# Token loads of the last operands: other tiles, ScalarE's queue, three groups

## The chip, the cores and the metric

One core of a Trainium2 chip runs the kernel. The metric is the device time of one execution in microseconds (us). TensorE (PE) multiplies, VectorE (DVE), ScalarE (ACT) and GpSimd (POOL) work on tiles in on-chip memory, and SyncE (SP) issues transfers (DMAs) between it and HBM. Each engine works through its own queue in order.

## What is computed

A decoder block on x of 2048 tokens by 1024, in fp32: a mixing layer (stick-breaking attention and pooling) and then a gated feed-forward layer. The change lies in the second:

```python
h = rmsnorm(x, g_ffn_pre[l]) * (1.0 + scale_f) + shift_f
f = (jax.nn.silu(h @ w_gate[l]) * (h @ w_up[l])) @ w_down[l]
x = x + gate_f * rmsnorm(f, g_ffn_post[l])
```

w_gate and w_up are 1024 by 2816, w_down is 2816 by 1024.

## The kernel before

Every fp32 product is made of three matmuls on fp32r pairs: a tile is split into a high part (ScalarE's cast) and a low part (VectorE's difference), and the three helper lines L72, L73, L74 multiply high by high, low by high and high by low. In most splits here (`split_by_bank`) ScalarE also copies the rounded value into a PSUM bank (L1176), and VectorE takes the low part from there (L1177).

The products with w_gate and w_up are two-level Strassen-like schemes of seven products each. Four *passes* (`inner`, q = 0 to 3, names p1 to p4) make some products for 11 column chunks j each; a chunk is seven steps of six matmuls, in the banks a, e, f, b, h, i, d. Their results go to HBM (`pd`, L1385). Then 11 *main* chunks (`gate_up`) follow, twelve steps of twelve matmuls each, which fetch the passes' products again (`px`, L1433) and add them. A main step's names: t2, t3 or b22 for the token operand (the trace prints t and b), 0 or 1 for the half of the tokens, g or u for gate or up. The first main chunk takes t2 of both halves (four steps), t3 of half 0, b22 of half 0, t3 of half 1 (`t31_g`, `t31_u`), b22 of half 1.

The main token operands are made beside pass four, in a side generator that gets one turn per step. `main_operands` loads, for each of eight row blocks u, three parts (n = 1, 3, 0) of the stored tokens h2d (`token_part`, L1622, 256 KB), subtracts and adds them on GpSimd (L1692) and splits the results into t2, t3 and b22 of half 0 and t2 of half 1. `rest_operands` loads parts 1 and 3 of the four row blocks of half 1, subtracts on GpSimd (L1726) and splits into t3 and b22 of half 1. Loaded tiles are named hs{block}_{i}_{n}: hs8_3_0 is part 0 of row block 3 of half 1; two tiles of `rest_operands` lie in one wide tile, hs_wide.

Scratch tiles have tags with a fixed number of buffers: "gs" has 3, "cu" 2, "v2", "v3", "u4" and "p1" one each ("u2", "v2", "u3", "v3" hold sums in the main chunks). A new tile of a tag waits until the readers of the one before are done. In pass four each chunk's gate weights come in two row halves, g and g2, that GpSimd adds (L1347).

The order of the compute engines' instructions is the program's own. SyncE's transfers are put in an order by the scheduler, which judges by its own model when a tile is free; the chip then follows that order strictly. Each transfer signals one of eight counters (DMAHW0 to DMAHW7), in turn over both issuing queues, and a transfer is issued only when the one before on its counter has landed.

## Time and profile before

| what | us |
|---|---|
| median of 3 runs (2202.04 to 2202.92) | 2202.14 |
| the profiled execution | 2203.83 |
| its span, first to last instruction | 2202.0 |
| TensorE busy in the span | 2172.7 |
| pass four, first to last step | about 1315 to 1413 |
| main chunks | 1414.6 to about 1765 |

Busy times are sums over instructions of one engine. An engine that is not the bound may be idle at no cost. A wait is put down to the instruction that released it last. In rows of a timeline stand the start, the duration, engine, line, operation, written tile, read tiles and the shape; in brackets the idle time ahead and its releaser. SPq rows are issues of transfers, not the transfers.

### The profile page before, as it was taken

The page shows a single profiled execution, that of the slowest core. Times are in us where ns is not written, and L with a number is a line of the kernel's source. Part 1 is how long each engine was busy: PE and PEld are TensorE (multiplying, and loading weights), DVE is VectorE, ACT ScalarE, POOL GpSimd, SP SyncE. Part 2 cuts the span into 40 slices and gives each one's busy share as a digit, 9 for nine tenths or more (in the row PEclk, how much of TensorE's full clock was granted, in tenths as well). Part 3 has the DMA queues.
Part 4 walks back from the last instruction along what each step waited for, and adds up shares of the span by engine and source line. Part 5 has one row for each costly group of instructions (what it writes and reads, how often), then busy time and mean ns, then how long its engine had stood idle before and what let it go on. Part 6 is the DMA issues. An engine that isn't in the chain of part 4 may idle for free.

```text
span 2202.0 us, 34273 instructions
## 1 busy us (share of the span) xinstructions
PE 2172.7 (99%) x10349; PEld 1796.3 (82%) x10349; DVE 1673.7 (76%) x2552; ACT 1356.3 (62%) x2796; POOL 1215.6 (55%) x1700
## 2 busy tenths in 40 slices
PE   8999999999999999999999999999999999999998
PEld 6888888888888888887878878788888888888887
DVE  7874499999999966547778878788778765577566
ACT  5334589989989854547766657554444444455444
POOL 1352267787879965547788677566666520032003
PEclk9999999999999999999999999999999999999999
DMA  8986886634343445668889889899999897679553
GB/s 315 335 290 208 285 218 176 172 90 119 113 136 97 149 163 193 196 216 286 287 297 334 271 273 285 276 337 327 302 314 297 308 323 259 211 245 327 187 199 118
DMA packets 365573, 524.78 MB, mean 238 GB/s; under 512 B 24198, under 2 KB 203978, under 8 KB 357836
## 3 DMA queue, kind: packets, MB, share of 16 engines
q1 hardware_dynamic: 362828, 521.02, 72.3%
q8 instruction: 82, 1.34, 0.3%
q10 hardware_dynamic: 2560, 1.58, 0.3%
q14 instruction: 103, 0.84, 0.1%
HBM read 350.01 MB, written 172.49 MB: 237 GB/s over the span
## 4 chain that ended last, share of the span: by engine, by line
PE 52%; POOL 2%; DVE 2%; DMA 1%; ACT 1%; issue 1%; SPq 0%; DVEq 0%; POOLq 0%; ACTq 0%
PE dn0p L74 3%; PE dn0p L73 3%; PE dn0p L72 3%; PE dn1p L73 3%; PE dn1p L72 3%; PE dn1p L74 3%; PE t_g L72 2%; PE t_u L72 2%; PE t_g L73 2%; PE t_u L73 2%; PE t_g L74 2%; PE t_u L74 2%; PE mix L72 1%; PE mix L73 1%; PE mix L74 1%
## 5 line engine op out<-in xcount | busy, mean ns | idle before, releaser
L953 POOL TENSOR_TENSOR w<-sg,pr 128x512 f32<-128x512 f32 (+2 forms) x320 | 306.3, 957 | 46.4 <-DVE pr L948 15.4
L948 DVE TENSOR_TENSOR_SCAN pr<-pr,carry,begin 128x512 f32<-128x512 f32 x192 | 244.0, 1271 | 0.0
L932 ACT ACTIVATE sg<-z 128x512 f32<-128x512 f32 (+2 forms) x320 | 183.7, 574 | 51.0 <-PE z L930 41.5
L63 DVE TENSOR_TENSOR wtl<-wt,wth 128x512 fp32r<-128x512 f32 (+1 forms) x320 | 189.6, 592 | 17.9 <-ACT wth L62 15.7
L62 ACT CAST wth<-wt 128x512 fp32r<-128x512 f32 (+1 forms) x320 | 183.0, 572 | 10.4 <-PE wt L964 10.4
L934 ACT ACTIVATE pr<-z 128x512 f32<-128x512 f32 (+2 forms) x320 | 183.2, 572 | 0.0
L964 PE MATMUL wt<-ident,w 128*128 128x128 f32 x1088 | 172.3, 273 | 1.6 <-POOL pr L944 1.1
L964 PEld LDWEIGHTS wt<-ident,w 128*128 128x128 f32 x1088 | 134.1, 140 | 32.8 <-POOL pr L944 1.9
L1486 ACT ACTIVATE sa<-sa 128x512 f32<-128x512 f32 x88 | 54.7, 632 | 160.8 <-DVE sa L1485 158.1
L979 PE MATMUL av<-wth,vt 128*128 128x512 f32 (+1 forms) x320 | 126.1, 394 | 0.9 <-ACT o L984 0.8
L63 DVE TENSOR_TENSOR g0p_l<-g0p,g0p_h 128x512 fp32r<-128x512 f32 x77 | 59.6, 775 | 79.8 <-ACT g0p_h L62 79.8
L73 PE MATMUL dn0p<-w0p_l,g0p_h 128*128 128x512 f32 x308 | 119.8, 389 | 0.0
L74 PE MATMUL dn0p<-w0p_h,g0p_l 128*128 128x512 f32 x308 | 119.8, 389 | 0.0
L72 PE MATMUL dn0p<-w0p_h,g0p_h 128*128 128x512 f32 x308 | 119.8, 389 | 0.0
L929 PE MATMUL z<-kt,qt 128*128 128x512 f32 (+2 forms) x320 | 118.7, 371 | 0.7 <-ACT pr L934 0.6
L980 PE MATMUL av<-wtl,vt 128*128 128x512 f32 (+1 forms) x320 | 117.8, 368 | 1.3 <-DVE wtl L63 1.2
L930 PE MATMUL z<-kt,qt 128*128 128x512 f32 (+2 forms) x320 | 116.9, 365 | 0.0
L73 PE MATMUL dn1p<-w1p_l,g1p_h 128*128 128x512 f32 x292 | 113.6, 389 | 0.0
L74 PE MATMUL dn1p<-w1p_h,g1p_l 128*128 128x512 f32 x292 | 113.6, 389 | 0.0
L72 PE MATMUL dn1p<-w1p_h,g1p_h 128*128 128x512 f32 x292 | 113.6, 389 | 0.0
L62 ACT CAST g0p_h<-g0p 128x512 fp32r<-128x512 f32 x77 | 48.0, 623 | 105.3 <-PE dn0p L73 92.5
L945 DVE TENSOR_TENSOR_SCAN pr<-pr,zero,begin 128x128 f32<-128x128 f32 (+3 forms) x128 | 111.2, 871 | 1.7 <-ACT pr L934 1.7
(852 smaller groups left out, 7151.6 us busy)
## 6 DMA issues: line engine op xcount, KB each, us to landing
pd<-p_c SPq DMA_DIRECT2D x176, 256.0 KB, 4.9
px<-pd SPq DMA_DIRECT2D x42, 1024.0 KB, 7.3
hs<-h2d SPq DMA_DIRECT2D x78, 256.0 KB, 4.7
wc<-in_w_cond_dram SPq DMA_DIRECT2D x32, 512.0 KB, 7.4
qt<-qd SPq DMA_DIRECT2D x64, 256.0 KB, 4.1
kt<-kd SPq DMA_DIRECT2D x96, 128.0 KB, 3.2
vt<-vd SPq DMA_DIRECT2D x48, 256.0 KB, 4.0
wd<-in_w_down_dram SPq DMA_DIRECT2D x44, 256.0 KB, 5.5
```

The source lines that it names most:

```text
L62: nc.scalar.copy(hi, src)
L63: low.tensor_tensor(lo, src, raw(hi), ALU.subtract)
L72: nc.tensor.matmul(ps, lh, rh, start=first and i == 0, stop=False)
L73: nc.tensor.matmul(ps, lh, rl, start=False, stop=False)
L74: nc.tensor.matmul(ps, ll, rh, start=False, stop=last and i == n - 1)
L929: nc.tensor.matmul(z[:, 0:L], qt[:, 0, i * P:(i + 1) * P], keys, start=True, stop=False)
L932: nc.scalar.activation(sg[:, 0:L], z[:, 0:L], AF.Sigmoid, scale=0.125)
L934: nc.scalar.activation(pr[:, 0:L], z[:, 0:L], AF.Sigmoid, scale=-0.125)
L948: nc.vector.tensor_tensor_scan(keys, keys, begin, carry, ALU.mult, ALU.bypass)
L953: nc.gpsimd.tensor_tensor(w[:, 0:L], sg[:, 0:L], pr[:, 1:L + 1], ALU.mult)
L964: nc.tensor.transpose(wt[:, i * P:(i + 1) * P], wss[u][i][:, b * P:(b + 1) * P], ident)
L979: nc.tensor.matmul(av[:, lo0:], vb, wh[:, lo0:], start=first, stop=False)
```

## The change

Three things are edited. The last chunk's gate halves of pass four go to the tiles v3 and v2 instead of the two "cu" tiles. The last row block of `main_operands` (u = 7) takes "cu", "cu" and "gs" instead of three "gs" tiles, and its part 0 is loaded by ScalarE. The eight loads of `rest_operands` are issued by ScalarE instead of SyncE, and in three groups (row blocks 0 and 1; 2; 3) instead of all at the start; one more turn is left free ahead of the last row block's subtraction.

```diff
                 if m == NQ * HF - 1:
-                    st["g"], st["g2"] = (ft("cu", f"{name}_{n}") for n in ("g", "g2"))
+                    st["g"], st["g2"] = (ft(tag, f"{name}_{n}") for n, tag in (("g", "v3"), ("g2", "v2")))
...
-    def token_part(n, T0, tag, i, t=None):
+    def token_part(n, T0, tag, i, t=None, queue=nc.sync):
         t = ft(tag, f"hs{T0}_{i}_{n}", (P, HK, P)) if tag else t
-        nc.sync.dma_start(t, h2d[T0 + n % 2 * HK + i][:, n // 2 * HK:(n // 2 + 1) * HK, :])
+        queue.dma_start(t, h2d[T0 + n % 2 * HK + i][:, n // 2 * HK:(n // 2 + 1) * HK, :])
...
-            raw[u, n] = token_part(n, u // HK * NTS, tag, u % HK)
+            raw[u, n] = token_part(n, u // HK * NTS, tag, u % HK, queue=nc.scalar if u == 7 and not n else nc.sync)
...
-            tags = ("cu", "cu", "v2") if u in (1, 3, 5) else ("gs",) * 3
+            tags = ("cu", "cu", "gs" if u == 7 else "v2") if u % 2 else ("gs",) * 3
...
-        for i, (tag, tag2) in enumerate((("cu", "gs"), (None, "gs"), (None, "gs"), ("u4", "p1"))):
-            b12.append(token_part(1, NTS, tag, i, wide[:, (i - 1) % 2]))
-            b22.append(token_part(3, NTS, tag2, i))
-        yield
-        yield
-        for k in range(HK + 2):
-            if k < HK:
+        tags = (("cu", "gs"), (None, "gs"), (None, "gs"), ("u4", "p1"))
+        for k in range(-2, HK + 2):
+            for i in {-2: (0, 1), -1: (2,), 1: (3,)}.get(k, ()):
+                b12.append(token_part(1, NTS, tags[i][0], i, wide[:, (i - 1) % 2], nc.scalar))
+                b22.append(token_part(3, NTS, tags[i][1], i, queue=nc.scalar))
+            if k == HK - 1:
+                yield
+            if 0 <= k < HK:
                 nc.gpsimd.tensor_tensor(b12[k], b22[k], b12[k], ALU.subtract)
```

SyncE's queue late in pass four, before. The rows are pass-four sums on their way out (pd), weights of pass four (p4_10) and of main chunk 0 (g_0), and token loads:

```order
L1334 DMA p4_10_g2_17960<-in_w_gate_dram 128x4x128
L1385 DMA pd0_158<-p4_6_c00_17853 128x512
L1385 DMA pd1_159<-p4_6_c11_17868 128x512
L1385 DMA pd0_158<-p4_6_c10_17885 128x512
L1622 DMA hs8_3_1_18076<-h2d15_135 128x512
L1622 DMA hs8_3_3_18078<-h2d15_135 128x512
L1445 DMA g_0_320_18010<-in_w_gate_dram 128x8x128
L1385 DMA pd1_159<-p4_6_c01_17923 128x512
L1340 DMA p4_10_32_17958<-in_w_up_dram 128x8x128
L1622 DMA hs8_0_1_18346<-h2d12_132 128x512
L1385 DMA pd0_158<-p4_7_c00_17971 128x512
L1385 DMA pd1_159<-p4_7_c11_17986 128x512
```

The same stretch now:

```order
L1622 DMA hs8_3_3_18078<-h2d15_135 128x512
L1385 DMA pd0_158<-p4_6_c00_17853 128x512
L1385 DMA pd1_159<-p4_6_c11_17868 128x512
L1385 DMA pd0_158<-p4_6_c10_17885 128x512
L1334 DMA p4_10_g2_17960<-in_w_gate_dram 128x4x128
L1445 DMA g_0_320_18010<-in_w_gate_dram 128x8x128
L1385 DMA pd1_159<-p4_6_c01_17923 128x512
L1340 DMA p4_10_32_17958<-in_w_up_dram 128x8x128
L1385 DMA pd0_158<-p4_7_c00_17971 128x512
L1385 DMA pd1_159<-p4_7_c11_17986 128x512
L1385 DMA pd0_158<-p4_7_c10_18002 128x512
```

The pair hs8_3_1, hs8_3_3 has gone ahead of the sums of chunk 6 (its first load stands four rows higher still), g2 has taken its place ahead of g_0, and hs8_0_1 and hs8_3_0 have left SyncE. The first gate half, p4_10_g, now stands some 350 rows higher, in pass one.

ScalarE at the start of main chunk 0, before (b0g0 and b0u0 copy products of px00 into banks; t3_1h is the high part of a row block of t3 of half 1; L1486 is the silu):

```order
L1176 COPY rounded_18338<-g_0_s3_h_18335 128x512
L1480 COPY b0g0_0_18390<-px00_0_18285 128x512
L1169 CAST u_0_s3_h_18398<-u_0_320_18057 128x512
L1176 COPY rounded_18401<-u_0_s3_h_18398 128x512
L1486 ACT_TABLE_LOAD
L1486 ACTIVATE sa110_0_18394<-sa110_0_18394 128x512
L1480 COPY b0u0_0_18419<-px00_0_18285 128x512
L1169 CAST t3_1h_18341<-hs8_0_1_18346 128x4x128
```

And now, with the counters that each row waits for:

```order
L1622 DMA hs8_0_1_18346<-h2d12_132 128x512 [waits DMAHW0_49]
L1622 DMA hs8_0_3_18348<-h2d12_132 128x512 [waits DMAHW4_49]
L1622 DMA hs_wide_18345<-h2d13_133 128x512 [waits DMAHW5_49]
L1622 DMA hs8_1_3_18351<-h2d13_133 128x512 [waits DMAHW7_49]
L1622 DMA hs_wide_18345<-h2d14_134 128x512 [waits DMAHW0_49]
L1622 DMA hs8_2_3_18366<-h2d14_134 128x512 [waits DMAHW2_49]
L1480 COPY b0g0_0_18386<-px00_0_18285 128x512 [waits DVE_49]
...
L1480 COPY b0u0_0_18415<-px00_0_18285 128x512 [waits DMAHW1_49]
L1622 DMA hs8_3_1_18421<-h2d15_135 128x512 [waits DMAHW6_49,DVE_49]
L1622 DMA hs8_3_3_18423<-h2d15_135 128x512 [waits DMAHW0_49]
L1169 CAST t3_1h_18341<-hs8_0_1_18346 128x4x128 [waits PE_49,Pool_49]
```

Six loads stand ahead of b0g0 and two ahead of the first cast of t3_1h. On the counters: hs8_0_1 has DMAHW2 (GpSimd's L1727 waits for it there), the first half of px00 has DMAHW0.

VectorE in chunk 0, before (t30_g and t30_u are the results of t3 of half 0; t3_1l and b22_1l the low parts of t3 and b22 of half 1):

```order
L1177 TENSOR_TENSOR u_0_s4_l_18488<-u_0_s4_18266,rounded_18490 128x512
L1177 TENSOR_TENSOR t3_1l_18342<-hs_wide_18345,rounded_18495 128x4x128
L63 TENSOR_TENSOR b22_1l_18344<-hs8_1_3_18351,b22_1h_18343 128x4x128
L1506 TENSOR_TENSOR t30_g_0_18466<-t30_g_0_18466,u2g0_0_18392 128x512
L1485 TENSOR_TENSOR sa120_0_18519<-t30_g_0_18466,px10_0_18372 128x512
L1485 TENSOR_TENSOR sa220_0_18521<-t30_g_0_18466,px10_0_18372 128x512
L1516 TENSOR_TENSOR u2g0_0_18392<-b1g0_0_18516,u2g0_0_18392 128x512
L1177 TENSOR_TENSOR t3_1l_18342<-hs8_3_1_18356,rounded_18525 128x4x128
```

And now:

```order
L1506 TENSOR_TENSOR t30_g_0_18466<-t30_g_0_18466,u2g0_0_18388 128x512
L1485 TENSOR_TENSOR sa120_0_18512<-t30_g_0_18466,px10_0_18368 128x512
L1485 TENSOR_TENSOR sa220_0_18514<-t30_g_0_18466,px10_0_18368 128x512
L1516 TENSOR_TENSOR u2g0_0_18388<-b1g0_0_18509,u2g0_0_18388 128x512
L1177 TENSOR_TENSOR t3_1l_18342<-hs_wide_18345,rounded_18519 128x4x128
L63 TENSOR_TENSOR b22_1l_18344<-hs8_1_3_18351,b22_1h_18343 128x4x128
L1506 TENSOR_TENSOR t30_u_0_18496<-t30_u_0_18496,u2u0_0_18417 128x512
L1512 TENSOR_TENSOR cu0_0_18544<-t30_u_0_18496,px10_0_18368 128x512
L1489 TENSOR_TENSOR t30_u_0_18496<-t30_u_0_18496,px10_0_18368 128x512
L1490 TENSOR_TENSOR sa220_0_18514<-sa220_0_18514,t30_u_0_18496 128x512
L1516 TENSOR_TENSOR u2u0_0_18417<-b1u0_0_18541,u2u0_0_18417 128x512
L1177 TENSOR_TENSOR t3_1l_18342<-hs8_3_1_18421,rounded_18551 128x4x128
```

The low part of row block 3 stood behind t30_g's sums; now it stands behind t30_u's five rows too.

## The prediction

> **What bounds the kernel now.** First the head of the page: who is busy, and for how long.

> ```profile
> span 2202.0 us, 34273 instructions
> PE 2172.7 (99%) x10349; PEld 1796.3 (82%) x10349; DVE 1673.7 (76%) x2552; ACT 1356.3 (62%) x2796; POOL 1215.6 (55%) x1700
> ```

> TensorE is idle for 2202.0 - 2172.7 = 29.3 us in all, so the change can win only what of this lies at its place. The profiled execution took 2203.83 us, 1.8 outside its span and 1.7 above the median 2202.14; I work with differences and add them to the median. 0.2% of it, 4.4 us, is about what a measurement of this kernel tells from no change.

> Second, TensorE's waits between 1360 and 1460 us (the end of pass four and the first main chunk), and its timeline there (start, duration, in brackets the idle time ahead):

> ```profile
> PE t_g L72 <- DVE p_c L1389: 1.5, 1, 1.5
> PE hp L72 <- DVE p_c L1389: 0.2, 1, 0.2
> ...
> 1409.48 0.39 PE L74 MATMUL bp<-yap4h,p_g_l 128*128 128x512 f32 x1
> 1410.05 0.47 PE L72 MATMUL hp<-v32p4h,p_s_h 128*128 128x512 f32 x1 [0.18 <-DVE p_c L1389]
> 1411.58 0.39 PE L72 MATMUL ip<-v14p4h,p_u_h 128*128 128x512 f32 x1
> 1412.72 0.39 PE L74 MATMUL ip<-v14p4h,p_u_l 128*128 128x512 f32 x1
> 1414.63 0.47 PE L72 MATMUL t_g<-t_0h,g_s_h 128*128 128x512 f32 x1 [1.53 <-DVE p_c L1389]
> 1417.46 0.39 PE L72 MATMUL dp<-y22p,p_s_h 128*128 128x512 f32 x1
> ```

> These two waits are the whole target. Starts without a wait are 0.227 us apart (1411.58 to 1412.72 is 5 of them). From 1409.48 to 1417.46 stand 25 matmuls, 5.68 us without a wait; they took 7.98. The most to be won is **2.30 us**, 0.10%.

> Third, the chain of waits through this place, and SyncE's queue:

> ```profile
> 1387.77 6.61 DMA p<-in_w_up_dram
> 1394.45 7.37 DMA g<-in_w_gate_dram
> 1401.95 1.29 POOL g L1451
> ...
> 1407.27 0.63 ACT t_1h L1169
> ...
> 1408.61 0.70 DVE t_1l L1177
> ...
> 1413.81 0.69 DVE p_c L1389
> ```
> ```profile
> 1373.58 0.65 SPq L1334 DMA_DIRECT2D p_g<-in_w_gate_dram  x1
> ...
> 1383.50 3.08 SPq L1622 DMA_DIRECT2D hs<-h2d  x2
> 1386.67 0.39 SPq L1445 DMA_DIRECT2D g<-in_w_gate_dram  x1
> ...
> 1405.89 1.69 SPq L1622 DMA_DIRECT2D hs<-h2d  x2
> 1407.67 0.39 SPq L1445 DMA_DIRECT2D u<-in_w_up_dram  x1
> ...
> 1413.49 1.30 SPq L1433 DMA_DIRECT2D px<-pd  x2
> ```

> SyncE's in-order queue is the cause: token loads that wait for their tiles (1383.50, 1405.89) hold the weight loads behind them. The gate weights of chunk 0 land at 1401.95, GpSimd's queue is late by that, the fourth row block's cast (L1169) with it, VectorE's low part at 1408.61 (L1177) holds the sums behind it, and the last of these (L1389, 1413.81) frees what t_g waits for.

> **The change, part by part.**

> *Row block 3 into other tiles, last gate weights into v3 and v2.* The pair of token loads now takes the place of the gate halves (1373.58), and the second half waits for v2, free some 3 us later. Nothing behind them waits for a token load any more; each load goes when VectorE has read its own tile, which for g, the one the chain runs through, is this row:

> ```profile
> 1389.21 0.68 DVE L1177 TENSOR_TENSOR p_g_l<-p_g,rounded 128x512 fp32r<-128x512 f32 x1
> ```

> So g goes near 1390 instead of 1394.45 and, with the same 7.4 us, lands at 1397.4; the up weights ahead of it (1387.77) go earlier still. The fourth row block is cast 4 to 5 us earlier, at about 1403, ahead of the sums it held. **-2.30 us**, both waits gone. The first gate half, free of any wait, moves to pass one in SyncE's order: one 0.4 us issue and 256 KB there; I cost it at nothing, and give +-1 us for the shift of the counters of all loads after it.

> *Token loads on ScalarE's queue.* Nine issues. The nearest rows: ScalarE's loads in pass one (issue in ns; then KB and us to landing), the landing of all loads of that line, of all token loads (4.7), of the token loads between 1400 and 1440 us, and of px; then a gap of ScalarE, and where GpSimd's queue stands:

> ```profile
> L1344 ACTq DMA_DIRECT2D p<-in_w_up_dram x2: 375/515/655, 1006.4 to 1017.0; - x2
> ...
> DMA to landing us min/median/max: 3.3/5.2/8.0
> ...
> p<-in_w_up_dram ACTq DMA_DIRECT2D x2, 256.0 KB, 6.0
> ...
> hs<-h2d SPq DMA_DIRECT2D x78, 256.0 KB, 4.7
> ...
> DMA to landing us min/median/max: 5.2/5.5/5.8
> ...
> px<-pd SPq DMA_DIRECT2D x4, 512.0 KB, 7.2
> ...
> 1394.94 0.59 ACT L1394 COPY p1p<-ap 128x512 f32<-128x512 f32 x1 [3.52 <-PE ap L74]
> ...
> 1408.43 1.30 POOL L1459 TENSOR_TENSOR g_s<-g,g 128x512 f32<-128x512 f32 x1 [1.20 <-PE fp L73]
> ```

> At about 0.4 us each: the one for row block 3 goes into the gap of 3.52 us ahead of 1394.94. Six stand ahead of b0g and two ahead of the first t3 cast. None is free there, because the queue behind each waits, and because the sixth, hs8_2_3, uses the counter of the first, hs8_0_1, and so waits until that has landed, with b0g (L1480) behind it. This is the new wait.

> ScalarE gets to the six at about 1414.7: g_s at 1408.43 keeps its wait for TensorE, then three GpSimd operations of 1.3 us (1412.3), then two casts with their copies, 2.4. If the first lands 4.7 us later (1419.4), the sixth issue ends at 1419.8 and VectorE's sa, behind b0g, starts 0.6 after: S = 1420.4. Bounds: the six issues alone, 2.3 us, S = 1417.6; a landing of 8.0, S = 1423.7. I take 4.7, the median of 78 loads of the same form, between ScalarE's 3.3 at best and its 6.0.

> *One step later.* In the new order the low part t3_1l of row block 3, the last that t31_g needs, stands behind five more VectorE rows. The rows of before:

> ```profile
> 1419.59 0.59 ACT L1480 COPY b0g<-px 128x512 f32<-128x512 f32 x1 [1.61 <-DMA px<-pd]
> ...
> 1420.21 0.69 DVE L1485 TENSOR_TENSOR sa<-b0g,px 128x512 f32<-128x512 f32 x1
> ...
> 1436.40 0.69 DVE L1177 TENSOR_TENSOR t_1l<-hs,rounded 128x512 fp32r<-128x512 f32 x1
> ...
> 1437.92 0.69 DVE L1506 TENSOR_TENSOR t_u<-t_u,u2u 128x512 f32<-128x512 f32 x1
> ...
> 1441.25 1.31 DVE L63 TENSOR_TENSOR b_1l<-hs,b_1h 128x512 fp32r<-128x512 f32 x1
> ...
> 1437.86 0.39 PE L72 MATMUL t_g<-t_1h,g_s_h 128*128 128x512 f32 x1
> ...
> 1420.00:1430.00 10.00, 10.00 (x46) 8.29 (x45) 8.54 (x15) 9.81 (x18) 1.67 (x2) 1.00 1.12 351
> ```

> Before, t3_1l ends at 1437.09, 16.88 us after sa's start and 0.77 before TensorE comes: that is all the slack. The five rows are those from 1437.92 to 1441.25, 3.33 us. So it now ends at S + 20.21. VectorE and ScalarE, busy 8.5 and 9.8 of 10 us there, give nothing back. TensorE, 2.30 earlier, wants it at 1437.86 - 2.30 + 0.23 = 1435.79 (the low part is read by the second matmul). The stall is S - 1415.6, the **net S - 1417.9**.

> *Sum.* -2.30 + (1420.4 - 1415.6) = -2.3 + 4.8 = **+2.5 us**: 2202.14 + 2.5 = 2204.6. Bounds: -0.3 (S 1417.6) to +5.8 (S 1423.7); -2.3 if the later place is covered.

> *What moves past what.* SyncE loses the nine issues, so px00 goes as soon as bp has read its tile, near 1409.8 instead of 1413.49; the 6 us it took (1413.49 to 1419.59) lets it land near 1416, ahead of S. px10, which b1g and sa wait for, lands near 1430: about 7.3 MB from 1409.8 at the 374 GB/s of the row below; it is wanted at about S + 12.4 = 1432.8, after the sums ahead of it. gf's load, now earlier in SyncE's order, waits for hs_wide's readers with only chunk-1 loads behind it, wanted 20 us later.

> ```profile
> 1400.00:1410.00 10.00, 9.87 (x44) 7.85 (x42) 4.41 (x8) 2.67 (x5) 6.42 (x5) 1.00 0.45 146
> 1410.00:1420.00 10.00, 8.43 (x36) 6.57 (x37) 7.57 (x13) 4.80 (x10) 6.95 (x6) 1.00 1.01 374
> ```

> These rows (last columns: clock, DMA share, GB/s) also say that six loads, 1.6 MB, move out of the half-empty stretch into the full one: 4.2 us of transfer at 374 GB/s. [...]

> **Rivals.**

> *Nothing is late next* (gain kept): if VectorE, less held up before 1420, has t3_1l early, the time is 2202.14 - 2.3 = 2199.8, at S = 1417.6 it is 2201.8. For it: the first part is well shown, and px comes 3.7 us earlier. Against it: it needs S below 1417.9, and the counter's wait stands ahead of b0g. Chance 0.20.

> *ScalarE held long* (slower): hs8_0_1 takes over 6.6 us to land, S passes 1422.3 and the net +4.4. At 8.0 it is +5.8, 2207.9. For it: DMA share 1.01, and 8.0 is the longest of L1344's loads; against it: token loads of this stretch took 5.2 to 5.8. Chance 0.18.

> *A cold TensorE* (slower): the forecast's stall of 4.8 us is three times the longest here (1.53, clock 1.00). If the clock halves after it, the 12 matmuls of t31_g take 0.454 each, +2.7, together +5.2: 2207.3. No row here shows it. [...] Chance 0.07.

> *The change doesn't do what it says*: t_g still waits, held by px or by ScalarE's casts, and the later place costs too: +2.5 to +4.8, within 0.2% mostly; it is part of the forecast's chance. A gain beyond 4.4 us has no waits here to come from; 0.03 for shifts in the other passes.

> **How the numbers follow.** Forecast (net 0 to +4.4) 0.52; gain kept 0.20; held long 0.18; cold 0.07; other gain 0.03. Within 0.2%: 0.52 + 0.20 = 0.72; slower 0.25; faster 0.03. Time 2204.6; range 2200.0 to 2208.0, from the kept gain to the long landing, leaves out under 0.2.

> **What would show it.** Right: no TensorE wait at the first t_g; chunk-0 gate weights landing before 1398; nine loads on ScalarE's queue, ScalarE idle ahead of b0g with a DMA as the releaser; a TensorE wait of 2 to 6 us at the first t_g that reads t_1, on VectorE's t_1l. Wrong: no such wait (then about 2200), a wait at the first t_g as before, or new waits in passes one to three.

## The result, and the profile after

The change makes the kernel slower: 2209.33 us median of 9 runs (2206.86 to 2212.17) against 2202.14 of before (9 runs beside them); the ratio is 1.0030 with a 95% interval of 1.0022 to 1.0039, +4.8 to +8.6 us. The forecast was 2204.6 us, with a range up to 2208.0. In eleven later runs it was 1.0024 (1.0015 to 1.0033). The profiled execution took 2208.09 us, 4.3 more than that of before; one lay 1.2 below its median and the other 1.7 above. The medians are 7.2 apart here and 4.8 in the later runs: the account below is of the 4.3, and why the first medians differ by more is not known.

TensorE's waits in the same part of the program, 1300 to 1520 us (us in total, times, longest):

```profile
PE t_g L73 <- DVE t_1l L1177: 2.6, 1, 2.6
PE t_g L72 <- ACT t_1h L1169: 2.1, 1, 2.1
```

Both waits of before, hp and the first t_g on p_c, are gone; two new ones stand at the first matmuls of t31_g. (A third wait of this view, 0.9 us at 1300, is the same in both kernels.) TensorE's timeline there:

```profile
1411.77 0.39 PE L72 MATMUL t_g<-t_0h,g_s_h 128*128 128x512 f32 x1
...
1434.67 0.39 PE L74 MATMUL b_u<-b_0h,u_s_l 128*128 128x512 f32 x1
1437.12 0.51 PE L72 MATMUL t_g<-t_1h,g_s_h 128*128 128x512 f32 x1 [2.07 <-ACT t_1h L1169]
1440.22 0.80 PE L73 MATMUL t_g<-t_1l,g_s_h 128*128 128x512 f32 x1 [2.60 <-DVE t_1l L1177]
1440.82 0.63 PE L74 MATMUL t_g<-t_1h,g_s_l 128*128 128x512 f32 x1
1441.24 0.63 PE L72 MATMUL t_g<-t_1h,g_s_h 128*128 128x512 f32 x1
1441.67 0.63 PE L73 MATMUL t_g<-t_1l,g_s_h 128*128 128x512 f32 x1
...
1444.78 0.40 PE L72 MATMUL t_u<-t_1h,u_s_h 128*128 128x512 f32 x1
1445.01 0.39 PE L73 MATMUL t_u<-t_1l,u_s_h 128*128 128x512 f32 x1
...
1452.97 0.39 PE L72 MATMUL t_g<-t_0h,g_s_h 128*128 128x512 f32 x1
```

t31_g could start at 1434.90, 2.96 us earlier than before (1437.86): the 2.30 of the two waits, and 0.66 by which this execution was ahead at 1300 already. It waits 4.67 us. Then the starts are 0.425 us apart instead of 0.227, until 1444.5. Chunk 1 starts at 1452.97 instead of 1448.74, 4.23 later, the whole difference of the two spans (4.3). Of this, -2.96 + 4.67 leaves 2.52 for the rest: the slow matmuls lose 2.10 of it (12.75 us for the 47 starts from 1440.22 to 1452.97, 10.65 for the same in the kernel before), and the two restarts 0.42. The granted clock (third column from the right) in four equal pieces of 3.41 us:

```profile
1434.15:1437.56 3.41, 1.34 (x5) 0.59 (x4) 3.38 (x6) 3.38 (x7) 1.28 (x1) 1.00 1.02 422
1437.56:1440.97 3.41, 0.81 (x3) 0.65 (x3) 3.31 (x7) 1.20 (x3) 3.25 (x3) 0.50 1.02 418
1440.97:1444.39 3.42, 3.42 (x10) 2.65 (x9) 2.79 (x4) 2.25 (x4) 1.39 (x2) 0.50 0.98 387
1444.39:1447.80 3.41, 3.41 (x17) 2.78 (x16) 2.79 (x5) 1.36 (x3) 3.34 (x3) 1.00 0.34 128
```

The clock fell behind a piece in which TensorE was busy for 1.34 of 3.41 us (first number behind the length), stayed at half for two pieces, and came back behind one in which it was busy throughout.

What made t31_g wait, from ScalarE's, VectorE's and SyncE's timelines:

```profile
1413.57 0.83 ACTq L1622 DMA_DIRECT2D hs<-h2d  x2
...
1417.60 0.33 ACTq L1622 DMA_DIRECT2D hs<-h2d  x1
1417.97 0.59 ACT L1480 COPY b0g<-px 128x512 f32<-128x512 f32 x1 [3.82 <-DMA hs<-h2d]
...
1432.68 0.59 ACT L1480 COPY b1g<-px 128x512 f32<-128x512 f32 x1 [2.80 <-DMA px<-pd]
```
```profile
1418.59 0.69 DVE L1485 TENSOR_TENSOR sa<-b0g,px 128x512 f32<-128x512 f32 x1 [3.04 <-ACT b0g L1480]
...
1432.69 1.29 DVE L1485 TENSOR_TENSOR sa<-t_g,px 128x512 f32<-128x512 f32 x2 [1.03 <-DMA px<-pd]
...
1439.49 0.68 DVE L1177 TENSOR_TENSOR t_1l<-hs,rounded 128x512 fp32r<-128x512 f32 x1
```
```profile
1414.11 0.38 SPq L1445 DMA_DIRECT2D g<-in_w_gate_dram  x1
...
1419.02 0.38 SPq L1445 DMA_DIRECT2D g<-in_w_gate_dram  x1
...
1423.69 0.55 SPq L1433 DMA_DIRECT2D px<-pd  x1
```

ScalarE holds b0g for 3.82 us (S = 1418.59); SyncE issues px10 only at 1423.69, it lands at 1432.68, and t3_1l ends at 1440.18. What SyncE's queue waited for between 1405 and 1425:

```profile
SPq L1445 <- DMA hs<-h2d: 3.2, 1, 3.2
SPq L1445 <- DMA px<-pd: 3.1, 1, 3.1
...
SPq L1445 <- DMA hs_wide<-h2d: 1.0, 1, 1.0
SPq L1385 <- DMA px<-pd: 0.8, 1, 0.8
SPq L1385 <- DMA hs<-h2d: 0.6, 1, 0.6
```

The token loads are no longer in SyncE's queue, yet its rows ahead of px10 wait for them: in the trace the gate load issued at 1419.02 signals the same counter as hs8_0_3, the up load behind it (1420.49) that of hs_wide, and pd (1421.48) that of hs8_1_3, all three issued by ScalarE. First come 3.1 and 0.8 us of waiting for px loads to land (before 1415.40), then the three for token loads, 4.8 us, up to px10's issue. The profiles of part1 and groups_sync (below) have none of these five waits.

### The profile page after: what moved, and what is told of

It reads as the page before. It is cut to its first block, busy times and chain, and to the rows that moved or that the text cites. A ratio compares the mean times of both kernels' runs of the same rounds, so it can differ in the third digit from the quotient of the medians.

```text
span 2206.3 us, 34258 instructions
## 1 busy us (share of the span) xinstructions
PE 2174.6 (99%) x10349; PEld 1797.5 (81%) x10349; DVE 1675.5 (76%) x2552; ACT 1357.1 (62%) x2796; POOL 1215.4 (55%) x1700
## 3 DMA queue, kind: packets, MB, share of 16 engines
q8 instruction: 82, 1.34, 0.3%
## 4 chain that ended last, share of the span: by engine, by line
PE 85%; DVE 5%; ACT 3%; POOL 3%; issue 2%; DMA 2%; SPq 0%; DVEq 0%; POOLq 0%; ACTq 0%
PE wt L964 4%; PE dn0p L72 3%; PE dn0p L73 3%; PE dn0p L74 3%; PE dn1p L72 3%; PE dn1p L73 3%; PE dn1p L74 3%; PE av L980 2%; PE z L929 2%; PE z L930 2%; PE av L979 2%; PE mix L72 2%; PE mix L74 2%; PE mix L73 2%; PE t_g L73 2%
## 5 line engine op out<-in xcount | busy, mean ns | idle before, releaser
L63 DVE TENSOR_TENSOR wtl<-wt,wth 128x512 fp32r<-128x512 f32 (+1 forms) x320 | 189.8, 593 | 17.8 <-ACT wth L62 15.7
L1486 ACT ACTIVATE sa<-sa 128x512 f32<-128x512 f32 x88 | 54.8, 632 | 170.4 <-DVE sa L1485 170.4
L63 DVE TENSOR_TENSOR g0p_l<-g0p,g0p_h 128x512 fp32r<-128x512 f32 x77 | 59.6, 774 | 79.7 <-ACT g0p_h L62 79.7
L72 PE MATMUL dn0p<-w0p_h,g0p_h 128*128 128x512 f32 x308 | 119.8, 389 | 0.0
L73 PE MATMUL dn0p<-w0p_l,g0p_h 128*128 128x512 f32 x308 | 119.8, 389 | 0.0
L74 PE MATMUL dn0p<-w0p_h,g0p_l 128*128 128x512 f32 x308 | 119.8, 389 | 0.0
L72 PE MATMUL dn1p<-w1p_h,g1p_h 128*128 128x512 f32 x292 | 113.6, 389 | 0.0
L73 PE MATMUL dn1p<-w1p_l,g1p_h 128*128 128x512 f32 x292 | 113.6, 389 | 0.0
L74 PE MATMUL dn1p<-w1p_h,g1p_l 128*128 128x512 f32 x292 | 113.6, 389 | 0.0
## 6 DMA issues: line engine op xcount, KB each, us to landing
pd<-p_c SPq DMA_DIRECT2D x176, 256.0 KB, 4.9
hs<-h2d SPq DMA_DIRECT2D x71, 256.0 KB, 4.6
wc<-in_w_cond_dram SPq DMA_DIRECT2D x32, 512.0 KB, 7.3
qt<-qd SPq DMA_DIRECT2D x64, 256.0 KB, 4.1
vt<-vd SPq DMA_DIRECT2D x48, 256.0 KB, 4.0
wd<-in_w_down_dram SPq DMA_DIRECT2D x44, 256.0 KB, 5.5
```

The source lines that it names most:

```text
L63: low.tensor_tensor(lo, src, raw(hi), ALU.subtract)
L72: nc.tensor.matmul(ps, lh, rh, start=first and i == 0, stop=False)
L73: nc.tensor.matmul(ps, lh, rl, start=False, stop=False)
L74: nc.tensor.matmul(ps, ll, rh, start=False, stop=last and i == n - 1)
```

## The experiments

Each was timed beside the kernel before, 9 to 11 times (px10_act 5 times); the ratio is to that one. "Wait" is TensorE's at t31_g in the profile, "clock" the lowest granted behind it.

| kernel | median us | ratio (95%) | wait us | clock |
|---|---|---|---|---|
| part1 | 2201.07 | 0.9992 (0.9983 to 1.0001) | 0 | 1.00 |
| part1_again | 2200.52 | 0.9991 (0.9982 to 0.9999) | 0 | 1.00 |
| groups_sync | 2200.36 | 0.9994 (0.9985 to 1.0003) | 0 | 1.00 |
| noyield | 2201.80 | 1.0000 (0.9992 to 1.0009) | 0.6 | 1.00 |
| part1_yield | 2203.62 | 1.0006 (0.9997 to 1.0015) | 1.9 | 1.00 |
| filler | 2205.24 | 1.0014 (1.0005 to 1.0022) | 0 | 1.00 |
| filler15 | 2205.49 | 1.0013 (1.0005 to 1.0022) | 2.3 | 0.50 |
| yield_filler | 2206.83 | 1.0019 (1.0010 to 1.0028) | 2.6 | 1.00 |
| filler10 | 2208.14 | 1.0022 (1.0013 to 1.0031) | 2.6 | 0.50 |
| yield_only | 2208.71 | 1.0026 (1.0017 to 1.0035) | 2.8 | 0.50 |
| sixth_sync | 2207.39 | 1.0029 (1.0020 to 1.0038) | 4.0 | 0.50 |
| sixth_px10 | 2209.09 | 1.0028 (1.0019 to 1.0038) | 5.4 | 0.50 |
| px10_act | 2210.40 | 1.0038 (1.0026 to 1.0051) | 4.6 | 0.50 |
| after_again | 2207.44 | 1.0024 (1.0015 to 1.0033) | 5.1 | 0.50 |

### Which part makes the wait

**noyield**, the changed kernel less one line:

```diff
-            if k == HK - 1:
-                yield
```

> The changed kernel without the extra free turn in rest_operands, all else kept (ScalarE still issues the loads, in the same groups). Theory A (the stall at t31_g comes from the order of VectorE's and ScalarE's rows, and the halved clock from the stall): VectorE waits for px10 until 1432.7 us as now, then three sums and t3_1l end near 1435.2, where TensorE wants it at 1435.1; no TensorE wait over 0.3 us, granted clock 1.00 in 1430 to 1448, time 2202.1 - 3.0 = 2199.2. Rival B (the loads on ScalarE's queue and their late landing hold t3_1): the two waits stay, 2 us or more, and the time is 2202 or more. Rival C (the loss sits elsewhere than in these waits): 2207 or more.

Measured: t3_1l one step earlier, a wait of 0.6 us (at most 0.3 was expected), the clock at 1.00, a span of 2198.8 (3.2 below before's); the median, 2201.80, is 0.8 below, where theory A had about 3. Rival C falls, and B as the only cause. The profile flatters this kernel: it is the shortest of its eleven runs, and its first t_g came at 1408.85, 2.1 us ahead of part1's. Three of the eleven lay above 2205; why is not settled.

**part1**, the kernel before with the first part alone:

```diff
-                    st["g"], st["g2"] = (ft("cu", f"{name}_{n}") for n in ("g", "g2"))
+                    st["g"], st["g2"] = (ft(tag, f"{name}_{n}") for n, tag in (("g", "v3"), ("g2", "v2")))
...
-            tags = ("cu", "cu", "v2") if u in (1, 3, 5) else ("gs",) * 3
+            tags = ("cu", "cu", "gs" if u == 7 else "v2") if u % 2 else ("gs",) * 3
```

with part 0 of row block 3 loaded by ScalarE, as in the change.

> The kernel before with the first part alone: last gate weights in v3 and v2, row block 3 in cu, cu, gs with its part 0 loaded by ScalarE; the eight other loads stay on SyncE, all issued at the start, and VectorE's order is that of before. Theory A: both waits ahead of the first t_g go, none comes at t31_g: 2199.2 to 2199.8. Rival E (the eight loads still hold SyncE's queue, so the up weights of chunk 0 and px00 are late in their place): some of the wait at the first t_g stays, 2200.5 to 2202.

Measured: no wait at the first t_g or t31_g, so theory A holds in its mechanism and rival E falls. The time is 1.5 us below before and falls short of theory A's (2201.07 against 2199.2 to 2199.8); the repeat shows about as much:

> The first part alone once more, beside its variant with the extra turn: 2201.1 us as in the first five rounds, 1.5 below the kernel before; if that gain was chance, 2202.1 to 2202.6.

1.9 below there. Against the kernel before this is a gain of under 0.1%, just clear of noise in the repeat and not in the first runs; against the changed kernel it is clear.

**yield_only**, the kernel before with the extra turn alone (the two lines of noyield added to it).

> The kernel before with the extra free turn alone: tiles and loads as before, all on SyncE. Theory A: t3_1l of row block 3 stands behind five more VectorE rows, 3.33 us, of which 0.77 is slack: a TensorE wait of 2.6 us at t31_g and 2204.7 us if the clock holds through a wait of this size, 2207.4 if it halves for the 12 matmuls behind it; the two waits before the first t_g stay. Rival B (ScalarE's queue is the cause, the order harmless): no wait at t31_g, 2202.1.

Measured: the wait forecast for this order (0.6 + 2.2 us, against 2.6), the halved clock, and 6.1 us: the free turn alone, with every load where it was, costs about what the whole change does, and rival B falls. Its clock in two stretches, the one before the fall and the low one:

```profile
1432.55:1435.96 3.41, 1.52 (x6) 0.70 (x4) 3.27 (x6) 3.18 (x6) 3.08 (x3) 1.00 1.02 423
1435.96:1442.79 6.83, 5.97 (x14) 4.77 (x15) 5.23 (x9) 2.25 (x4) 4.80 (x4) 0.50 0.90 365
```

It does not follow that the order suffices in the changed kernel: with the first part in, TensorE comes earlier, but so do px and VectorE. **part1_yield** is part1 with the extra turn:

> part1 (the first part alone, eight loads on SyncE at the start) with the extra free turn added: the late order without ScalarE's loads. Theory A2 (the wait at t31_g is made of two delays that share one slack): counted from the first t_g, t3_1l of row block 3 ends at 20.2 us in part1 and TensorE wants it at 23.4, so 3.2 us are spare; the loads on ScalarE take 3.9 of them (noyield, 24.05), the late order 4.3 (the changed kernel, 28.4, against noyield). Then it ends here at 24.5: a wait of about 1.2 us, too short for the clock (1.5 us in the kernel before left it at 1.00), and 2201.1 + 1.2 = 2202.3 us. Rival F (the order alone makes the long wait, as yield_only seemed to say): a wait of 3 us or more, halved clock, 2206 or more.

Measured 1.2 us above before, 3.1 above part1 beside it, with a wait of 1.9 us (1.2 were expected) and the clock at 1.00: rival F falls. The profile is the second shortest of its eleven runs; whether the clock fell in longer ones is not known. And **groups_sync** undoes ScalarE's queue alone in the changed kernel:

```diff
-                b12.append(token_part(1, NTS, tags[i][0], i, wide[:, (i - 1) % 2], nc.scalar))
-                b22.append(token_part(3, NTS, tags[i][1], i, queue=nc.scalar))
+                b12.append(token_part(1, NTS, tags[i][0], i, wide[:, (i - 1) % 2]))
+                b22.append(token_part(3, NTS, tags[i][1], i))
```

> The changed kernel with the eight loads of rest_operands on SyncE, all else kept: the three groups, the extra turn, the tiles (part 0 of row block 3 stays on ScalarE). Only the issuing queue is undone. Theory A3 (ScalarE's six loads delay b0g and all behind it by about 4 us, and that uses up the slack which the late order needs): S comes about 3 us after the first t_g instead of 6.8, the wait at t31_g is at most 2 us, as in part1_yield, the clock holds, 2202 to 2204 us. Rival K (it is the grouping, later loads, on whichever queue; here row block 3's pair stands on SyncE behind px10): waits of 3 us or more, halved clock, 2206 or more.

No wait at all, 2200.36 us, better than expected: with SyncE issuing the same three groups, the late order costs nothing, and rival K falls. Its VectorE and SyncE:

```profile
1414.70 0.68 DVE L1485 TENSOR_TENSOR sa<-b0g,px 128x512 f32<-128x512 f32 x1
...
1433.32 0.68 DVE L1177 TENSOR_TENSOR t_1l<-hs,rounded 128x512 fp32r<-128x512 f32 x1
```
```profile
1414.21 0.38 SPq L1445 DMA_DIRECT2D g<-in_w_gate_dram  x1
...
1418.29 0.38 SPq L1433 DMA_DIRECT2D px<-pd  x1
```

Counted from the first t_g of each kernel (1411.02 here, 1411.77 in the change), and with TensorE wanting t3_1l at 23.4:

| kernel | loads issued by | order | S | px10 issued | t3_1l ends |
|---|---|---|---|---|---|
| part1 | SyncE | early | 3.7 | 9.7 | 20.2 |
| groups_sync | SyncE, groups | late | 3.7 | 7.3 | 23.0 |
| part1_yield | SyncE | late | 3.7 | 9.7 | 25.3 |
| noyield | ScalarE, groups | early | 6.9 | 12.3 | 24.1 |
| the change | ScalarE, groups | late | 6.8 | 11.9 | 28.4 |

The queue takes 5.4 us (28.4 - 23.0), the order 4.3 (28.4 - 24.1). About 3 are spare, so with the first part in, either alone makes TensorE wait 0 to 2 us and the two together 5.

**Inside ScalarE's queue.** Two runs took away one holder each, a third both:

> The changed kernel with one of the six loads ahead of b0g, hs8_2_3, issued by SyncE, so that ScalarE no longer waits for hs8_0_1 to land. Theory A2: b0g goes 2 us earlier, VectorE's sa, the last pass-four sums, px10's load and t3_1l follow, and the TensorE waits at t31_g come down from 4.7 to about 2.7 us; the clock still halves; 2209.3 - 2 = 2207.3. Rival G (px10's landing holds t3_1l and has nothing to do with ScalarE's wait): waits of 4.7 us as now, 2209.

Here S came as expected (4.7 after the first t_g), but px10 was issued and landed as late as in the change (20.7 after the first t_g), and 0.7 us of the wait went. The median is 2207.39, but the ratio to before is that of the change.

> The changed kernel with px10's load issued by ScalarE behind the six token loads, near 1418 us, instead of by SyncE at 1423.7. Theory A3 (two limits of nearly the same height hold t3_1l: px10's landing, and ScalarE's loads ahead of b0g through S; taking away one leaves the other): px10 lands by 1428, S comes 0.4 us later for the issue, t3_1l ends 20.2 us behind S, that is 27.4 us after the first t_g instead of 28.4, the TensorE waits at t31_g are 3.7 us instead of 4.7, the clock still halves, 2208.3 us. Rival G (px10's landing alone holds it): the waits fall to about 1 to 2 us, the clock holds, 2203 to 2204.

A miss: one load more on ScalarE made it hold b0g for 5.4 us instead of 3.8 and the first t3 cast for 3.7 instead of 0.8, and the time rose. Beside 4.6 us at t31_g, TensorE waited 2.1 in the two steps ahead (b22 of half 0), for low and high parts of weights. px10 was no longer late (VectorE's sums did not wait for it), yet t3_1l was, so rival G falls too.

> Both: hs8_2_3 issued by SyncE, and px10 by ScalarE, here just behind b0g and a cast with its copy, so that neither b0g nor px10 is held. Theory A3: S is 4.7 us after the first t_g (6.8 in the changed kernel), t3_1l ends at 24.9 to 25.3, the waits at t31_g are 1.5 to 2.0 us, the clock holds (it did at 1.9 us in part1_yield), 2202.5 to 2203.5 us. Rival H (the late order or GpSimd's queue, where row block 3's subtraction stands behind the late hs8_2_3, holds it at the old place): waits of 3 us or more, halved clock, 2206 or more.

S 4.7, but waits of 5.4 us: rival H. GpSimd's subtraction for row block 2 waited 9.7 us, until 1432.76, for hs8_2_3, which SyncE issued only at 1423.16 and which took 9.5 us to land; row block 3's stands behind it (ScalarE's casts of t_1h waited 1.9 and 0.9 us for GpSimd). How the 5.4 us of the queue divide between b0g's hold and px10's is therefore not settled; each load that was moved became somebody else's wait.

### The clock

**filler** puts idle work where TensorE waits:

```diff
+                if j == 0 and (n, kind, sb) == ("s3", "g", 1):
+                    for k in range(20):
+                        nc.tensor.matmul(ps, wst["s4r"][0][:, k % HK, :], ops[0]["b22"][0][:, k % HK, :], start=True, stop=True)
                 mm3(ps, [((wh[:, k, :], wl[:, k, :]), (th[:, k, :], tl[:, k, :])) for k in range(HK)])
```

> The changed kernel with 20 matmuls of idle work (b22 high by gate high, into t31_g's own bank, which the first real matmul then starts afresh) ahead of t31_g: 20 x 0.227 = 4.54 us, about as long as the two waits of 4.67 us. Theory A: TensorE stays busy, the granted clock stays 1.00, and the 2.5 us of slow matmuls after the waits are gone: time = before - 3.0 + 4.7 to 4.9 = 2203.9 to 2204.1. Rival D (the low clock there has nothing to do with idleness, or does not cost time): the time stays at 2208 to 2209.5.

Measured 2205.24 (2203.9 to 2204.1 were expected), +2.6 against before and 2.2 to 4.1 below the changed kernel (its two medians), with more matmuls to run. Its clock:

```profile
1430.00:1436.00 6.00, 6.00 (x28) 4.99 (x27) 5.28 (x9) 5.16 (x10) 1.55 (x2) 1.00 1.07 414
1436.00:1442.00 6.00, 6.00 (x27) 4.68 (x26) 5.79 (x10) 3.13 (x6) 4.01 (x3) 1.00 1.01 412
```

So here the low clock came with TensorE's waits (0.50 with 4.67 us of them, 1.00 with none) and cost time; rival D falls. **yield_filler** does the same to yield_only, with 13:

> yield_only (the kernel before with the extra turn) with 13 idle matmuls (2.95 us) ahead of t31_g, where it waited 2.75 us. If 3.4 of the 6.1 us that yield_only lost are the clock, as theory A says (2.7 late, 12 to 15 matmuls at half speed), the clock stays at 1.00 and the time is 2205.2 to 2205.6, 3 us below yield_only's 2208.7. If the lateness alone makes the loss: 2208 to 2209.

Here px10 came late (21.7 us after the first t_g; 19.5 in yield_only), so 2.6 us of waiting stayed; the clock held nevertheless, and the median is 1.9 below yield_only's instead of 3.

```profile
1436.36 0.42 PE L72 MATMUL t_g<-t_1h,g_s_h 128*128 128x512 f32 x1
1439.35 0.50 PE L73 MATMUL t_g<-t_1l,g_s_h 128*128 128x512 f32 x1 [2.56 <-DVE t_1l L1177]
1439.69 0.40 PE L74 MATMUL t_g<-t_1h,g_s_l 128*128 128x512 f32 x1
```

**filler10** and **filler15** are filler with 10 and 15:

> The changed kernel with 10 idle matmuls (2.27 us) ahead of t31_g instead of 20: about 2.4 us of waiting stay, nearly all in one piece behind t31_g's first matmul. If the clock halves whenever a stretch of about 3.4 us is less than half busy (in the changed kernel it fell 2.5 us after TensorE went idle, with one matmul in between, and came back 6.8 us later; in yield_only 2.4 and 6.7 us), it falls here in part of the executions only: 2204.5 to 2207.5, and 0.50 or 1.00 in the profiled one. If idleness has to last over 3.4 us, or the sum of the waits decides, the clock stays at 1.00 and the time is that of the 20 matmuls, 2205.2.

> The changed kernel with 15 idle matmuls (3.4 us) ahead of t31_g, between the 10 that left a wait of 2.6 us and a clock of 0.50 in its profile, and the 20 that left none. About 1.5 us of waiting stay, or 2 where px10 lands late. If the clock needs a stretch of some 3.4 us less than half busy, it holds: 1.00, and 2205.2 us as with 20. If any wait of 1.5 us behind a late operand brings it down here: 0.50 and 2207 or more.

Both profiles have a clock of 0.50, in one piece of 3.41 us. The medians are 2208.14 (2204.21 to 2209.90; above the expected 2204.5 to 2207.5) and 2205.49 (2203.20 to 2208.27); filler15's profile is the longest of its eleven runs, so most of its executions lost less than this one. filler10's low piece, and filler15, whose wait ended at 1440.29:

```profile
1440.58:1443.99 3.41, 3.01 (x7) 2.43 (x8) 3.31 (x6) 1.79 (x4) 2.09 (x2) 0.50 1.03 425
```
```profile
1441.09 0.40 PE L73 MATMUL t_g<-t_1l,g_s_h 128*128 128x512 f32 x1
1441.32 0.56 PE L74 MATMUL t_g<-t_1h,g_s_l 128*128 128x512 f32 x1
1441.68 0.63 PE L72 MATMUL t_g<-t_1h,g_s_h 128*128 128x512 f32 x1
```
```profile
1437.98:1441.39 3.41, 1.10 (x5) 0.93 (x6) 3.31 (x7) 0.94 (x2) 3.41 (x3) 1.00 1.04 423
1441.39:1444.81 3.42, 3.42 (x10) 2.65 (x9) 2.77 (x5) 2.25 (x4) 1.39 (x2) 0.50 0.97 390
```

In filler15 the clock fell 1.1 us after work had resumed. A wait of 2.56 us left it alone in one execution, one of 2.31 brought it down in another: its length alone does not decide.

**after_again** and **after_look** (a profile alone) are the changed kernel:

> The changed kernel once more, beside these two: 2209.3 us; waits of 4.7 us at t31_g and a clock of 0.50 for 6.8 us, as in the first profile, if what follows a long wait is always the same. If it depends on how the wait falls into a fixed rhythm of the clock's own, the time at 0.50 differs from the first profile by some us, in steps of about 3.4, and the loss with it.

> A third profile of the changed kernel, for the length of the time at 0.50 and its place against the wait: 6.8 us from 2.5 us after TensorE went idle if it is always the same, another place and 3.4 or 6.8 us if the rhythm is the clock's own.

Waits of 5.1 and 5.2 us, the clock at half for 6.8 us in both, from 2.5 and 3.8 us after TensorE's last matmul had ended (2.5 in the first profile). The length repeats, the place does not. The falls of one profile keep a rhythm that the wait does not set: in the change the clock fell at 24.45, 48.34, 1437.56 and 2202.15 us, 7, 407 and 224 pieces of 3.4133 us apart (1389.22 / 407); in before at 24.03, 47.92 and 2198.32 us, 7 and 630 of these pieces apart. All are whole to 0.01 us.

Cut into these pieces, the profiles agree. At t31_g the clock fell in nine, behind pieces with 0.39 (px10_act) to 1.52 us (yield_only) of TensorE's work; it held in before behind one with 2.04 (from 1413.26), and past the first 60 us in before and in the change behind all that were busier. filler15's wait of 2.31 us lay in one piece, with 1.10 of work. By the same figures, an estimate, yield_filler's of 2.56 lay across two: one piece with all of it would have had 3.41 - 2.56 = 0.85 us of work, and with 0.39 to 1.52 the clock fell in the nine. Only the two falls in the first 60 us came behind busier pieces (3.07 and 3.41 us in the change, 3.21 and 3.41 in before); their cause stays open.

## Why the prediction was wrong, point by point

- **Both waits of before go: right.** g was issued at 1389.3 (about 1390 was forecast) and the fourth row block cast at 1400.2 (1403). Of the 2.30 us, part1 shows 1.5 and 1.9 in its medians.
- **ScalarE waits for the first load behind its sixth: right**, with S at 1418.59 instead of 1420.4.
- **px10 lands near 1430: wrong**, 1432.68. The forecast took its transfer from the bandwidth and did not follow SyncE's queue through the counters that it shares with ScalarE's loads (4.8 us of waiting for them).
- **Five more VectorE rows ahead of t3_1l: right** (the late order took 4.3 us), **but it ends 21.59 us behind S, not 20.21**: VectorE waited 1.03 us for px10. That S was 1.8 early and this 1.4 late is luck: they nearly cancel, 1440.18 against 1440.6.
- **A stall of 4.8 us: right in size**, 4.67, but in two waits: 2.07 for ScalarE's cast of t3_1h, which the prediction left out, and 2.60 for t3_1l. The slack that it gives for t3_1l, 0.77, is that of the first matmul; by the second, which its sum uses, it is 1.00. That filler, with TensorE kept busy, comes to +2.6 where the sum has +2.5 is partly chance: filler itself was forecast at 2203.9 to 2204.1 and took 2205.24.
- **The step that failed is the rival of the cold TensorE**, given a chance of 0.07, the author's estimate with no run behind it. The clock fell in all three profiles of the changed kernel and in all others with a wait over 2.6 us. By the pieces above, an estimate: a wait longer than 2 x (3.41 - 1.52) = 3.8 us cannot escape, because one of the pieces it touches keeps at most 1.52 us of work; so by it the forecast's own stall, 4.8 us, had to bring the clock down. "No row here shows it" holds for the fall behind a stall, not for the clock: the profile of before has it at 0.50 from 24.03 and from 47.92 us, 3.41 us each. No row of the prediction shows its 0.454 us for a matmul at half the clock; in the change the starts were 0.425 apart. The price, 2.7, was about right (2.1 by the starts, 2.52 with the restarts); it belonged in the sum, which with it is the prediction's own 2207.3.
- **Rivals.** "Nothing is late next" needed S below 1417.9 and is what groups_sync does, on SyncE. "ScalarE held long" did not come: it needed S past 1422.3, and S was 1418.59.

That ScalarE issued the loads gained nothing here: groups_sync, with the eight back on SyncE, has a median of 2200.36 us, the change 2209.33 and, in the later runs, 2207.44.

## What to carry to other kernels

A wait of TensorE can cost more than its length: behind the 4.67 us in the change, matmuls at a clock of 0.50 lost 2.10 more. By these runs, as an estimate, a wait under 3.41 - 2.04 = 1.37 us leaves the clock alone if TensorE is busy around it, one over 3.8 brings it down, and between them it depends on where the wait falls: look at the granted clock behind it in pieces of a few us, and add the matmuls at half speed to the sum. The loads moved to ScalarE's queue held that engine's own work here (b0g, 3.82 us), and through shared completion counters the queue that they left as well (SyncE, 4.8 us); follow both queues to the next transfer that somebody needs. Two delays that share one slack are to be tried together: with the first part in, each alone made TensorE wait 0 to 2 us here, both 5.
